# Four single PSUM banks in place of two double ones after the attention, in a one-core attention + RWKV-7 + FFN layer

## The chip, the cores and the metric

One core of one Trainium2 chip runs the whole layer as one program. The metric is the device time of that program in microseconds (us), the median of several runs. TensorE is called PE, VectorE DVE, ScalarE ACT, GpSimd POOL, and SP issues the DMAs.

## The reference

One layer over 16 meta tokens and 1024 inputs (1040 positions, width 1024), all in float32:

```python
def hybrid_mixer(hn, ...):
    q, k, v, f_logit, rw, gates = split(hn @ w_in)
    o_fox  = fox_attention(norm(q), norm(k), v, cumsum(log_sigmoid(f_logit)))   # 8 heads of 64
    y      = rwkv7_scan(r, decay, k, v, -kk, kk * a)                            # 8 heads of 64
    o_rwkv = (group_norm(y) + bonus) * g
    g_fox, g_rwkv = split(sigmoid(gates + g_b))
    return (g_fox * (o_fox @ w_bf) + g_rwkv * (o_rwkv @ w_br)) @ w_o

def conv_ffn(hn, w_up, w_conv, w_down):           # D_FF = 2816, conv of width 3 along time
    gate, val = split(causal_conv(hn @ w_up))
    return (silu(gate) * val) @ w_down

h = h + hybrid_mixer(rms_norm(h), ...);  h = h + conv_ffn(rms_norm(h), ...)
```

## The kernel before

**Data.** Activations lie transposed, 128 features on the partitions and time along the free axis, 1026 columns in three pieces (`CW`) of 342. To keep float32 accuracy each product is three matmuls of a rounded form (`mm3`, lines 212 to 220): high weight times high data, high weight times low data, low weight times high data. A product with 1024 inputs is 24 matmuls into one PSUM bank, called a group here; with 512 inputs 12. `wload` (line 194) fetches a weight tile `wf` of 256 KB, ACT rounds it to `wh` (line 205), POOL subtracts to get `wl` (line 206).

**Stages.** Stage 0 makes the projections. Then three streams are merged (`stage12`): `att` (attention, queries in blocks, whose scores need 1024 columns in one piece), `rec` (preparation, then the scan: 17 chunks of 64 steps, `rw_chain`) and `gat` (the gate projections, in three pieces for each of 16 weight tiles, written to DRAM as `sg`). A chunk is a chain on small tiles: eight products from the state `zb` (line 522), copy `pt` (ACT, 524), eight products (533), copies `uv` (ACT 534 and DVE 535), eight products (540), the next state (DVE, 543); sixteen products give the output (548, 550), which goes to DRAM as `y_d` (copy `yt`, 552). Each chunk loads the next one's tensors (`rw_load`): w, am and bkt of 256 KB and six of 64 KB, 1,152 KB. Gate products fill PE between the links. After the scan the third piece's group norm (`group_norm`, four times: a product with `bo64` at line 872, a square on ACT, a second product at line 877, and a chain to `orw`) and the load of the attention's result (`fox_load`, `ofx`) run beside stage 3, which makes `merged`. Stage 4 multiplies by `w_o`, adds the input and takes the norm: a sum over partitions (line 623), fourteen small DVE steps, a broadcast by PE into `st` (line 638), and per 128 features a scaled `x` (DVE, 1033), its rounding (ACT, 1035) and its rest (DVE or POOL, 1036). It does so for pieces 0 and 1, then for piece 2. Stage 5 makes for each of 22 tiles three column pieces of `ug` and `uv` (`conv`: a group, then ACT 1075 and DVE 1076 and 1077, all three reading the bank; then ACT 1088, DVE 1090, ACT 1092, POOL 1093) and, in between, the down products `dn` (512 columns).

**PSUM.** There are 8 banks of 512 float32 columns. The pool `S.pp` holds the tags S and M, each of two banks (1024 columns), and t, o, A and B of one. `banks(S, mm="S S M M t")` names the places that a kind of use takes in turn; `psum` (line 238) hands out the next. Two equal names in a row are the two halves of one tile, which is taken once for both:

```python
    if n and slots[n - 1] == t:
        return S.half[tag][:, 512:1024]
    S.half[tag] = slot(S, t, tag)
    return S.half[tag][:, 0:512]
```

So before, the gates run on S S M M, stage 3 on S S M M t o A, stages 4 and 5 on S S M M t; `gn` has t and o, `ch` A and B, `st` and `dn` o, A and B. Attention needs S and M whole.

**Order.** A scheduler orders each engine's instructions by a simulated timeline, with the order of the program as priority; it may move a group, or part of one, ahead of another where it thinks that the first would wait. A change of places thus changes the order as well.

Of the kernel before, what the change touches and what calls it, by code (L numbers as in the profile page):

```python
# [7 lines left out]
F32 = mybir.dt.float32  # L8
# [6 lines left out]
PSUM = bass.MemoryType.PSUM  # L15
DRAM = bass.MemoryType.DRAM

P = 128
# [208 lines left out]
def banks(S, **use):  # L227

    S.psb.update({k: v.split() for k, v in use.items()})
    S.psn.update({k: 0 for k in use})  # L230


def slot(S, tag, name):
    w = 1024 if tag in "SM" else 512
    return S.pp.tile([P, w], F32, name=name, tag=tag, bufs=1)


def psum(S, tag):

    slots = S.psb[tag]  # L240
    n = S.psn[tag] % len(slots)
    S.psn[tag] += 1
    t = slots[n]
# [4 lines that stand above are left out]
# [642 lines left out]
def stage12(S):  # L890

    nc, tc = S.nc, S.tc
    banks(S, mm="S S M M", st="t o", pr="A B", t="t", o="o")
    p1_cm = tc.tile_pool(name="p1", bufs=1, side="right")
    p1 = p1_cm.__enter__()
    S.smask = p1.tile([P, 384], BF16, name="smask")
    nc.gpsimd.memset(S.smask[:], 1.0)
    nc.gpsimd.memset(S.smask[:].rearrange("p (c t) -> p c t", t=64)[:, :, 0:1], 0.0)
    stage0(S)
    banks(S, mm="S M")  # L900
    S.op = S.rp = None
    S.scanned = False
    S.ev = 0

    def att():
        with tc.tile_pool(name="a", bufs=1) as ap:
            forget(S, ap)
            yield 12
            S.q2 = [[ap.tile([66, 348], F32R, name=f"q2{i}{e}") for e in range(2)] for i in range(3)]
            for i in range(3):  # L910
                for e in range(2):
                    nc.gpsimd.memset(S.q2[i][e][64:66, :].bitcast(F32), 1.0)
            for p in range(NP_):
                yield from attention(S, ap, p)
        S.op_cm = tc.tile_pool(name="op", bufs=1)
        S.op = S.op_cm.__enter__()
        S.orw = [[S.op.tile([P, LT], F32R, name="orw", bufs=8) for _ in range(2)] for _ in range(4)]
        banks(S, gate="S S M M", gn="t o", ch="A B", sv="A B")

    def rec():  # L920
        yield from prep(S, p1)
        p1_cm.__exit__(None, None, None)
        with tc.tile_pool(name="r", bufs=1, side="right") as rp:
            S.rp = rp
            banks(S, sv="A", ch="A", gate="B")
            if S.op is not None:
                banks(S, gate="S S M M", ch="A B", sv="A B")
            two = lambda nm: [[rp.tile([P, 4, 64], F32, name=f"{nm}{i}{e}") for e in range(2)] for i in range(2)]

            S.zb, S.arb = two("zb"), two("arb")  # L930
            for e in range(2):
                nc.gpsimd.memset(S.zb[0][e][64 * e:64 * e + 64], 0.0)
                for i in range(2):
                    nc.gpsimd.memset(S.arb[i][e][64 - 64 * e:128 - 64 * e], 0.0)
            S.at = {}
            yield from solve(S, 0)
            nxt = iter(())
            for c in range(NCH):
                if c % 6 == 0:
                    yield from nxt  # L940
                    nxt = solve(S, c // 6 + 1) if c < 12 else iter(())
                for t in rw_chain(S, c):
                    yield t
                    for _ in range(2):
                        next(nxt, None)
                if c in (5, 10):
                    while S.op is None:
                        yield 1.0
                    yield from group_norm(S, (5, 10).index(c))

        S.of_cm = tc.tile_pool(name="of", bufs=1, side="right")
        S.ofp = S.of_cm.__enter__()
        S.scanned = True
        yield from merge_streams([(0.0, 1.0, group_norm(S, 2)), (0.0, 1.0, fox_load(S))])

    def gat():
        while S.rp is None:
            yield 1.0
        yield from gates(S, range(13))

        while not S.scanned:
            yield 1.0
        yield from gates(S, range(13, 16))

    for _ in merge_streams([(0.0, 1.0, att()), (0.0, 1.2, rec()), (0.0, 1.0, gat())]):
        pass
# [17 lines left out]
def stage3(S):  # L984

    nc, tc = S.nc, S.tc
    banks(S, mm="S S M M t o A")
    op = S.ofp
    T = lambda name, bufs=1: op.tile([P, 342], F32, name=name, tag=name, bufs=bufs)
    S.mg = []  # L990
    sgs = {}

    def branch(m, br):
        wb = wload(S, S.A["w_br"][8 * br + m], 4)
        if len(S.mg) <= m and (m, 1 - br, 0) in sgs:
            S.mg.append([S.xp.tile([P, LT], F32R, name=nm, tag="x") for nm in ("mh", "ml")])
        for c, (t0, t1) in enumerate(CW):
            o = slice(t0 - T0, t1 - T0)
            ot = (S.ofox, S.orw)[br]
            sg = sgs[m, br, c] = T("sg", 12)  # L1000
            nc.sync.dma_start(out=sg[:], in_=S.sg_d[8 * br + m, :, o])
            nc.scalar.activation(out=sg[:], in_=sg[:], func=AF.Tanh, scale=0.5)  # L1002
            ps = psum(S, "mm")
            mm3(S, ps[:, :342], wb, [(ot[k][0][:, o], ot[k][1][:, o]) for k in range(4)])
            nc.vector.scalar_tensor_tensor(out=sg[:], in0=sg[:], scalar=1.0, in1=ps[:, :342],
                                           op0=ALU.add, op1=ALU.mult)
            mf = sgs.get((m, 1 - br, c))
            if mf is not None:
                h, l = S.mg[m]
                nc.vector.tensor_tensor(out=mf[:], in0=mf[:], in1=sg[:], op=ALU.add)  # L1010
                nc.scalar.activation(out=h[:, o], in_=mf[:], func=AF.Copy, scale=0.5)
                nc.vector.scalar_tensor_tensor(out=l[:, o], in0=mf[:], scalar=0.5, in1=h[:, o], op0=ALU.mult, op1=ALU.subtract)


    for m, br in [(0, 0), (1, 0), (0, 1), (1, 1)] + [(m, br) for m in range(2, KD) for br in range(2)]:
        branch(m, br)
    S.of_cm.__exit__(None, None, None)
    S.op_cm.__exit__(None, None, None)


def stage4(S):

    nc, tc = S.nc, S.tc
    banks(S, mm="S S M M t", st="o A B")
    S.h2 = [S.mp.tile([P, LT], F32, name="h2", tag="h", bufs=8) for _ in range(KD)]
    S.x2 = [[S.mp.tile([P, LT], F32R, name="x2", tag="x2", bufs=16) for _ in range(2)] for _ in range(KD)]
    with tc.tile_pool(name="p4", bufs=1) as p4:
# [10 lines left out]
        for cs in ((0, 1), (2,)):  # L1038
            acc = {}
            for m in range(KD):  # L1040
                w = wload(S, S.A["w_out"][m], KD)
# [14 lines left out]
            for c in cs:  # L1056
                st = psum(S, "st")
# [4 lines left out]
def stage5(S):  # L1062

    nc, tc = S.nc, S.tc
    banks(S, mm="S S M M t", dn="o A B")
    with tc.tile_pool(name="p5", bufs=1) as p5:

        def conv(w, mt, a, z, name):
# [52 lines left out]
def build(tc, A, outs):  # L1121
    S = K()
    S.nc = nc = tc.nc
    S.tc, S.A = tc, A
    with ExitStack() as ctx:
        cp = ctx.enter_context(tc.tile_pool(name="cst", bufs=1))
        dp = ctx.enter_context(tc.tile_pool(name="dram", bufs=1, space=DRAM))
        S.wp = ctx.enter_context(tc.tile_pool(name="w", bufs=1))
        S.xp = ctx.enter_context(tc.tile_pool(name="x", bufs=16))
        S.cp = cp  # L1130
        S.ar_d = dp.tile([NCH, P, 4, 64], F32, name="ar_d")
        S.w1_d = dp.tile([NCH, P, 8, 64], F32, name="w1_d")
        S.am_d = dp.tile([NCH, P, 8, 64], F32, name="am_d")
        S.a_d = dp.tile([3, NCH, 8, 32, 32], F32, name="a_d")
        S.x_d = dp.tile([2, NCH, 8, 32, 32], F32, name="x_d")
        S.bkt_d = dp.tile([NCH, P, 512], F32, name="bkt_d")
        S.v_d = dp.tile([LP, 512], F32, name="v_d")
        S.g_d = dp.tile([4, P, L], F32, name="g_d")
        S.bon_d = dp.tile([4, P, L], F32, name="bon_d")
        S.sw_d = dp.tile([4, P, L], F32, name="sw_d")  # L1140
        S.tha_d = dp.tile([4, P, L], F32, name="tha_d")
        S.y_d = dp.tile([4, P, L], F32, name="y_d")
        S.sg_d = dp.tile([16, P, LT], F32, name="sg_d")
        S.f_d = dp.tile([8, 2, L], F32, name="f_d")
        S.of_d = dp.tile([4, P, L], F32, name="of_d")
        S.outT = outs
        S.psb, S.psn, S.half = {}, {}, {}
        S.pp = ctx.enter_context(tc.tile_pool(name="ps", bufs=1, space=PSUM))
        stage12(S)
        stage3(S)  # L1150
        S.mp = ctx.enter_context(tc.tile_pool(name="mf", bufs=1))
        stage4(S)
        stage5(S)
# [81 lines left out]
```

## Time and profile before

| | |
|---|---|
| median of 3 runs | 1974.12 us (1974.03 to 1975.23) |
| the profiled execution: time, span | 1975.84 us, 1974.1 us |
| PE busy | 1851.5 us, 94% of the span |
| DVE, ACT, POOL busy | 884.0, 729.7, 604.6 us |
| mean granted PE clock | 0.968 |
| stage 0 and attention, about | 0 to 690 us |
| scan with gates, about | 690 to 965 us |
| end of the scan to stage 3 | 965 to 1025 us |
| stage 3 / stage 4 / stage 5, about | 1025, 1150, 1208 to 1974 us |

PE is busy nearly throughout, so what counts is the time in which PE stands still or runs at its lower clock. In a row of the timeline the bracket gives how long the engine was idle before the instruction and what ended that. Matmuls overlap: their starts, not their durations, say how fast they follow one another.

### The profile page before, as it was taken

How to read it: one execution, taken by the hardware profiler on the slowest of the kernel's cores; microseconds unless marked ns; L12 is line 12 of the kernel's file. 1: busy time of each engine (PE TensorE's matmuls, PEld its weight loads, DVE VectorE, ACT ScalarE, POOL GpSimd, SP SyncE). 2: the span in 40 equal slices, each digit the busy share in tenths (PEclk: the TensorE clock that was granted, in tenths of full speed). 3: DMA queues.
4: the chain of work that ended last, by engine and by line, in shares of the span. 5: the costliest groups of instructions: out<-in, count | busy, mean ns of one | idle time of the engine just before them, and what ended most of it. 6: DMA issues, size and time to landing. Idle time of an engine off the chain costs nothing.

```text
span 1974.1 us, 33238 instructions
## 1 busy us (share of the span) xinstructions
PE 1851.5 (94%) x12876; PEld 1660.5 (84%) x12876; DVE 884.0 (45%) x1804; ACT 729.7 (37%) x1608; POOL 604.6 (31%) x651
## 2 busy tenths in 40 slices
PE   6899998999998999999789998999999999999999
PEld 5588788788786788888679988898988989989997
DVE  6125636636727686333155465332332332433333
ACT  5335535436535432334454334331331322322221
POOL 5134124124225212233222343332332332322322
PEclk9899998999998999999989998999999999999999
DMA  5221331323412537666535331111111111111113
GB/s 186 85 70 44 84 93 47 80 74 85 102 50 68 136 87 193 162 187 178 162 97 150 110 125 60 39 50 47 43 48 38 44 56 41 54 48 38 49 44 106
DMA packets 197574, 170.82 MB, mean 87 GB/s; under 512 B 93768, under 2 KB 155768, under 8 KB 197416
## 3 DMA queue, kind: packets, MB, share of 16 engines
q1 hardware_dynamic: 197160, 168.62, 30.1%
q8 instruction: 102, 1.67, 0.4%
q14 instruction: 56, 0.46, 0.1%
q0 software_dynamic: 256, 0.07, 0.0%
HBM read 122.57 MB, written 46.06 MB: 85 GB/s over the span
## 4 chain that ended last, share of the span: by engine, by line
PE 44%; DVE 3%; ACT 2%; DMA 1%; issue 1%; POOL 0%; SPq 0%; POOLq 0%; ACTq 0%; DVEq 0%
PE mm L218 11%; PE mm L219 11%; PE mm L220 10%; PE dn L218 4%; PE dn L220 4%; PE dn L219 4%; DMA sg<-sg_d 0%; DVE uv L1076 0%; DMA y<-of_d 0%; POOL wl L206 0%; DVE ug L1076 0%; ACT L652 0%; DVE ry L633 0%; DVE x L1033 0%; ACT L1002 0%
## 5 line engine op out<-in xcount | busy, mean ns | idle before, releaser
L206 POOL TENSOR_TENSOR wl<-wf,wh 128x512 fp32r<-128x512 f32 (+1 forms) x268 | 347.0, 1298 | 592.6 <-ACT wh L205 583.7
L218 PE MATMUL mm<-x,wh 128*128 128x344 f32 (+1 forms) x1056 | 339.7, 323 | 12.7 <-DVE uv L1077 8.3
L219 PE MATMUL mm<-x,wh 128*128 128x344 f32 (+1 forms) x1056 | 340.4, 323 | 0.6 <-DVE x L1036 0.5
L220 PE MATMUL mm<-x,wl 128*128 128x344 f32 (+1 forms) x1056 | 335.9, 322 | 1.6 <-POOL wl L206 1.6
L205 ACT CAST wh<-wf 128x512 fp32r<-128x512 f32 (+1 forms) x268 | 163.7, 612 | 380.6 <-PE dn L219 168.6
L218 PEld LDWEIGHTS mm<-x,wh 128*128 128x128 f32 x1056 | 200.9, 190 | 16.9 <-issue 12.5
L219 PEld LDWEIGHTS mm<-x,wh 128*128 128x128 f32 x1056 | 200.9, 190 | 2.0 <-DVE x L1036 1.2
L220 PEld LDWEIGHTS mm<-x,wl 128*128 128x128 f32 x1056 | 200.2, 190 | 2.5 <-POOL wl L206 2.4
L1104 DVE TENSOR_TENSOR h<-h,dn 128x512 f32<-128x512 f32 x96 | 65.9, 688 | 168.9 <-PE dn L220 168.8
L218 PE MATMUL dn<-gh,wh 128*128 128x512 f32 x352 | 138.5, 394 | 0.1
L219 PE MATMUL dn<-gl,wh 128*128 128x512 f32 x352 | 138.5, 394 | 0.0
L220 PE MATMUL dn<-gh,wl 128*128 128x512 f32 x352 | 138.3, 394 | 0.0
L1093 POOL TENSOR_TENSOR gl<-ug,gh 128x342 fp32r<-128x342 f32 (+1 forms) x66 | 57.8, 877 | 254.5 <-ACT gh L1092 244.8
L218 PE MATMUL gate<-xh,wh 128*128 128x342 f32 x384 | 128.3, 337 | 2.9 <-ACT sg L855 2.2
L219 PE MATMUL gate<-xl,wh 128*128 128x342 f32 x384 | 125.8, 328 | 0.0
L220 PE MATMUL gate<-xh,wl 128*128 128x342 f32 x384 | 124.2, 326 | 0.0
L1076 DVE SCALAR_TENSOR_TENSOR ug<-mm,par,ug 128x342 f32<-128x342 f32 (+1 forms) x66 | 37.7, 572 | 186.3 <-ACT ug L1075 186.3
L218 PE MATMUL mm<-xh,wh 128*128 128x348 f32 (+5 forms) x336 | 117.1, 349 | 4.0 <-ACT xh L156 1.9
L219 PE MATMUL mm<-xl,wh 128*128 128x348 f32 (+5 forms) x336 | 114.4, 340 | 3.3 <-POOL xl L158 3.1
L220 PE MATMUL mm<-xh,wl 128*128 128x348 f32 (+5 forms) x336 | 112.8, 336 | 0.0
L1076 DVE SCALAR_TENSOR_TENSOR uv<-mm,par,uv 128x342 f32<-128x342 f32 (+1 forms) x66 | 37.5, 573 | 139.7 <-ACT uv L1075 139.4
L218 PE MATMUL pr<-xh,wh 128*128 128x386 f32 (+1 forms) x288 | 96.2, 334 | 1.4 <-ACT bt L468 1.4
(306 smaller groups left out, 4031.5 us busy)
## 6 DMA issues: line engine op xcount, KB each, us to landing
wf<-in_w_up_dram SPq DMA_DIRECT2D x88, 256.0 KB, 2.7
sg_d<-sg SPq DMA_DIRECT2D x48, 171.0 KB, 4.1
sg<-sg_d SPq DMA_DIRECT2D x48, 171.0 KB, 2.6
wf<-in_w_gate_dram SPq DMA_DIRECT2D x32, 256.0 KB, 3.8
wf<-in_w_out_dram SPq DMA_DIRECT2D x32, 256.0 KB, 2.8
wf<-in_w_down_dram SPq DMA_DIRECT2D x32, 256.0 KB, 2.7
wf<-in_w_rw_dram SPq DMA_DIRECT2D x28, 256.0 KB, 2.8
wf<-in_w_qkv_dram SPq DMA_DIRECT2D x24, 256.0 KB, 2.8
```

The lines of the kernel that those rows point to most:

```text
L205: nc.scalar.copy(out=wh[:, :n], in_=wf[:, :n])
L206: nc.gpsimd.tensor_tensor(out=wl[:, :n], in0=wf[:, :n], in1=wh[:, :n], op=ALU.subtract)
L218: nc.tensor.matmul(ps, lhsT=wh, rhs=xh, start=first and k == 0, stop=False)
L219: nc.tensor.matmul(ps, lhsT=wh, rhs=xl, start=False, stop=False)
L220: nc.tensor.matmul(ps, lhsT=wl, rhs=xh, start=False, stop=last and k == n - 1)
L1076: nc.vector.scalar_tensor_tensor(out=t[:, :n], in0=ps[:, 1:1 + n], scalar=cw(1), in1=t[:, :n], op0=ALU.mult, op1=ALU.add)
L1093: nc.gpsimd.tensor_tensor(out=gl[:, s], in0=g[:, :n], in1=gh[:, s], op=ALU.subtract)
L1104: nc.vector.tensor_tensor(out=hs, in0=hs, in1=ps[:], op=ALU.add)
```

## The change

S and M leave the pool `S.pp` for a pool of their own, `ps1`, which is closed when the attention stream ends. A pool `ps2` is opened in its stead, with four tags 0, 1, 2, 3 of 512 columns. From there on every use that had S S M M has 0 1 2 3: gates, stage 3 (0 1 2 3 t o A), stages 4 and 5 (0 1 2 3 t). No instruction of the kernel's work is added or removed. Lines of the changed file lie one to five further down.

```diff
 def slot(S, tag, name):
     w = 1024 if tag in "SM" else 512
-    return S.pp.tile([P, w], F32, name=name, tag=tag, bufs=1)
+    pool = S.pp if tag in "toAB" else S.pq
+    return pool.tile([P, w], F32, name=name, tag=tag, bufs=1)
...
+    pq_cm = tc.tile_pool(name="ps1", bufs=1, space=PSUM)
+    S.pq = pq_cm.__enter__()
...
             for p in range(NP_):
                 yield from attention(S, ap, p)
+        pq_cm.__exit__(None, None, None)
+        S.pq = S.ctx.enter_context(tc.tile_pool(name="ps2", bufs=1, space=PSUM))
...
-        banks(S, gate="S S M M", gn="t o", ch="A B", sv="A B")
+        banks(S, gate="0 1 2 3", gn="t o", ch="A B", sv="A B")
...
-                banks(S, gate="S S M M", ch="A B", sv="A B")
+                banks(S, gate="0 1 2 3", ch="A B", sv="A B")
...
-    banks(S, mm="S S M M t o A")
+    banks(S, mm="0 1 2 3 t o A")
...
-    banks(S, mm="S S M M t", st="o A B")
+    banks(S, mm="0 1 2 3 t", st="o A B")
...
-    banks(S, mm="S S M M t", dn="o A B")
+    banks(S, mm="0 1 2 3 t", dn="o A B")
```

What it does to the order shows in three places. The first is stage 5, ACT, the middle of a typical tile (mm_13983 and so on are PSUM tiles; two names after one tile, as ug_14069 and uv_14038 from mm_14013, are its two halves). Before:

```order
L1075 ACTIVATE uv_14038<-mm_14013,par_133 128x340
L1092 CAST gh_13981<-ug_14008 128x340
L1075 ACTIVATE uv_14099<-mm_14074,par_133 128x342
L1075 ACTIVATE ug_14069<-mm_14013,par_133 128x342
L205 CAST wh_14169<-wf_14167 128x512
L1088 ACTIVATE ug_14069<-ug_14069 128x342
```

and in the changed kernel:

```order
L1080 ACTIVATE ug_14068<-mm_14043,par_136 128x340
L1093 ACTIVATE ug_14068<-ug_14068 128x340
L1080 ACTIVATE uv_14098<-mm_14073,par_136 128x340
L1097 CAST gh_14041<-ug_14068 128x340
L1080 ACTIVATE ug_14130<-mm_14105,par_136 128x342
L1093 ACTIVATE ug_14130<-ug_14130 128x342
L1080 ACTIVATE uv_14160<-mm_14135,par_136 128x342
```

Before, the uv of the second column piece (uv_14099) is read out ahead of its ug (ug_14069), which is the second half of mm_14013; now ug and uv come strictly by turns, each from a bank of its own, and on PE the groups stand whole, one after the other, to the end of the program.

The second place is PE at the last norm of stage 4, which stands among the first groups of stage 5 (mm_13206, mm_13267). Before:

```order
L219 MATMUL mm_13206<-x2_12018,wh_13127 128x344
L220 MATMUL mm_13206<-x2_12017,wl_13128 128x344
L623 MATMUL st_13059<-ones_137,acc_12759 114x1 x3
L218 MATMUL mm_13206<-x2_12019,wh_13127 128x344
L219 MATMUL mm_13206<-x2_12020,wh_13127 128x344
L220 MATMUL mm_13206<-x2_12019,wl_13128 128x344
L638 MATMUL st_13059<-ident_135,ry_13064 128x114 x3
```

Changed, around the second of the two products (line 639 there):

```order
L219 MATMUL mm_13257<-x2_12060,wh_13177 128x344
L220 MATMUL mm_13257<-x2_12059,wl_13178 128x344
L639 MATMUL st_13109<-ident_138,ry_13114 128x114 x3
L218 MATMUL mm_13287<-x2_12045,wh_13183 128x344
L219 MATMUL mm_13287<-x2_12046,wh_13183 128x344
```

Between the two products of the norm stood 3 matmuls, and now stand 41 (the last 17 of one group and the 24 of mm_13257).

The third place is ACT at the end of the scan (pt, uv0 and yt are links of the chain, sg is the read-out of a gate group). Before, chunks 15 and 16:

```order
L524 COPY pt_10319<-ch_10310 128x256
L205 CAST wh_11064<-wf_11062 128x512
L855 ACTIVATE sg_10908<-gate_10856,par_133 128x342
L855 ACTIVATE sg_10948<-gate_10923,par_133 128x342
L534 COPY uv0_10186<-ch_10351 64x256
L552 COPY yt_10390<-ch_10373 128x256
L205 CAST wh_11120<-wf_11118 128x512
L524 COPY pt_10402<-ch_10393 128x256
L855 ACTIVATE sg_10975<-gate_10923,par_133 128x342
L205 CAST wh_11187<-wf_11185 128x512
L855 ACTIVATE sg_11003<-gate_10978,par_133 128x342
L534 COPY uv0_10296<-ch_10433 64x256
```

and changed:

```order
L856 ACTIVATE sg_11029<-gate_11004,par_136 128x342
L553 COPY yt_10312<-ch_10295 128x256
L525 COPY pt_10338<-ch_10329 128x256
L535 COPY uv0_10205<-ch_10371 64x256
L553 COPY yt_10410<-ch_10393 128x256
L525 COPY pt_10422<-ch_10413 128x256
L535 COPY uv0_10315<-ch_10453 64x256
```

The last gate group is read out in chunk 14, and on PE no gate matmul stands between the links of chunks 15 and 16. In the chunks ahead of these, PE has up to 60 gate matmuls per chunk where it had about 48.

## Rows read from the trace of the kernel before

**Rows 1.** The page's busy times by engine, and the shares of the chain that ended last.

```profile
PE 1851.5 (94%) x12876; PEld 1660.5 (84%) x12876; DVE 884.0 (45%) x1804; ACT 729.7 (37%) x1608; POOL 604.6 (31%) x651
...
PE 44%; DVE 3%; ACT 2%; DMA 1%; issue 1%; POOL 0%; SPq 0%; POOLq 0%; ACTq 0%; DVEq 0%
```

**Rows 2.** Windows by stage: from:to, length, then busy us (and instructions) of PE, PE's weight loads, DVE, ACT, POOL, then granted PE clock, DMA share, GB/s.

```profile
0.00:690.00 690.00, 623.02 (x4324) 523.67 (x4324) 366.07 (x812) 321.82 (x792) 224.85 (x306) 0.94 0.32 86
690.00:965.00 275.00, 266.15 (x3076) 236.29 (x3076) 131.25 (x304) 90.74 (x205) 74.92 (x81) 0.99 0.59 160
965.00:1025.00 60.00, 39.60 (x218) 32.96 (x217) 26.86 (x56) 39.81 (x71) 11.28 (x12) 0.87 0.47 137
...
1150.00:1218.00 68.00, 58.33 (x340) 54.97 (x338) 49.50 (x108) 28.80 (x57) 32.88 (x27) 0.92 0.32 102
1218.00:1620.00 402.00, 390.85 (x2235) 368.25 (x2236) 131.11 (x229) 115.11 (x223) 120.67 (x107) 0.99 0.15 45
1620.00:1974.00 354.00, 349.48 (x1919) 320.83 (x1917) 118.12 (x196) 88.24 (x171) 100.06 (x90) 1.00 0.17 54
```

**Rows 3.** The waits of PE from 1240 to 1960 us (stage 5): what waited for what, us in total, times, longest.

```profile
PE mm L218 <- DVE uv L1077: 8.3, 6, 1.8
PE mm L220 <- POOL wl L206: 1.6, 2, 0.8
PE mm L218 <- DVE ug L1077: 1.4, 5, 0.5
```

**Rows 4.** The timeline at one of the longest of these waits: start, us, what, and the idle time before.

```profile
1270.48 1.02 ACT L1075 ACTIVATE uv<-mm,par 128x340 f32<-128x340 f32 x2 [2.87 <-PE mm L220]
...
1271.06 1.05 DVE L1076 SCALAR_TENSOR_TENSOR uv<-mm,par,uv 128x340 f32<-128x340 f32 x2 [3.97 <-ACT uv L1075]
1272.03 1.04 DVE L1077 SCALAR_TENSOR_TENSOR uv<-mm,par,uv 128x340 f32<-128x340 f32 x2
1272.74 0.40 PE L218 MATMUL mm<-x,wh 128*128 128x344 f32 x1 [1.82 <-DVE uv L1077]
```

**Rows 5.** The timeline from stage 4 into stage 5, the norm of the third piece and the first wait behind it.

```profile
1203.06 0.67 PE L623 MATMUL st<-ones,acc 128*114 128x1 f32 x6
...
1206.54 0.92 PE L638 MATMUL st<-ident,ry 114*128 114x114 f32 x6 [2.24 <-DVE ry L633]
1207.50 1.53 DVE L1033 SCALAR_TENSOR_TENSOR x<-h,par,st 128x342 f32<-128x342 f32 x3 [1.02 <-PE st L638]
...
1214.72 1.19 POOL L1036 TENSOR_TENSOR x<-x,x 128x342 fp32r<-128x342 f32 x1
```

**Rows 6.** PE's idle times in stage 4 and behind it, in the timeline.

```profile
1174.99 0.92 PE L638 MATMUL st<-ident,ry 114*128 114x114 f32 x6 [0.75 <-DVE ry L633]
...
1181.41 0.42 PE L218 MATMUL mm<-mh,wh 128*128 128x342 f32 x1 [2.19 <-ACT wh L205]
...
1182.95 0.42 PE L220 MATMUL mm<-mh,wl 128*128 128x342 f32 x1 [0.97 <-POOL wl L206]
...
1208.63 0.65 PE L218 MATMUL mm<-x,wh 128*128 128x344 f32 x1 [1.17 <-ACT x L1035]
...
1218.20 0.63 PE L218 MATMUL mm<-x,wh 128*128 128x342 f32 x1 [1.66 <-DVE ug L1077]
```

**Rows 7.** Windows around the stretches of a lower clock (columns as in rows 2).

```profile
1034.00:1184.00 150.00, 145.23 (x925) 143.76 (x924) 85.71 (x159) 58.24 (x118) 55.16 (x42) 1.00 0.42 127
1184.00:1191.00 7.00, 7.00 (x37) 6.81 (x36) 5.44 (x11) 4.32 (x9) 5.06 (x5) 0.76 0.44 138
...
1208.00:1225.00 17.00, 14.16 (x58) 12.96 (x59) 9.67 (x20) 8.49 (x16) 4.62 (x4) 0.71 0.10 31
...
1436.00:1443.00 7.00, 7.00 (x35) 7.00 (x36) 1.16 (x3) 1.66 (x4) 3.07 (x3) 0.76 0.08 27
```

**Rows 8.** Two matmuls of one group in a row at the lower clock, and two at full clock: start, us.

```profile
1436.56 0.49 PE L218 MATMUL mm<-x,wh 128*128 128x344 f32 x1
1436.85 0.49 PE L219 MATMUL mm<-x,wh 128*128 128x344 f32 x1
...
1443.30 0.32 PE L218 MATMUL mm<-x,wh 128*128 128x344 f32 x1
1443.46 0.32 PE L219 MATMUL mm<-x,wh 128*128 128x344 f32 x1
```

**Rows 9.** The links of a chunk near the scan's end, in the timeline.

```profile
954.19 0.68 PE L533 MATMUL ch<-pt,at 64*64 64x64 f32 x16
...
955.45 0.43 DVE L535 COPY uv<-ch 64x256 f32<-64x256 f32 x1 [6.01 <-ACT uv L534]
...
962.84 0.69 PE L522 MATMUL ch<-zb,w 128*64 128x64 f32 x16
963.63 0.37 ACT L524 COPY pt<-ch 128x256 f32<-128x256 f32 x1 [0.63 <-PE ch L522]
```

**Rows 10.** The third piece's norms on PE between the scan and stage 3, in the timeline.

```profile
999.16 1.13 PE L872 MATMUL gn<-y,bo 128*128 128x342 f32 x2 [4.38 <-DMA y<-y_d]
1005.15 0.74 PE L877 MATMUL gn<-sq,bo 128*128 128x342 f32 x2
1013.30 0.84 PE L872 MATMUL gn<-y,bo 128*128 128x342 f32 x2 [0.83 <-DMA y<-y_d]
...
1016.79 0.74 PE L877 MATMUL gn<-sq,bo 128*128 128x342 f32 x2
```

More of the change, by code (lines that the diff above doesn't have):

```diff
@@ L1125, in build @@
     with ExitStack() as ctx:
+        S.ctx = ctx
         cp = ctx.enter_context(tc.tile_pool(name="cst", bufs=1))
```

## The prediction

> **What bounds the kernel now.** Read first the busy times: PE works in 94% of the span, no other engine in half of it, and PE has 44% of the chain, DVE 3% [rows 1]. So the time is PE's work plus the places where PE stands still or runs at its lower clock, and a change that alters no instruction of the work can only move those. The windows by stage show where: the scan has 266.15 busy of 275 us, the stretch behind it 39.60 of 60, stage 4 with the way into stage 5 58.33 of 68, stage 5 some 11 idle in its first 400 us and 4.5 in the rest [rows 2]; not all of that is a wait, since some matmul records are missing, so the waits view is taken for sizes: in stage 5 PE waits 8.3 us in six waits for the last read-out of a uv, 1.4 in five for that of a ug, 1.6 in two for a low weight [rows 3]. The timeline shows what such a wait is: PE ends a group, ACT, DVE and DVE again read it (two pieces at a time, about 0.5 us each), and only then, 1.82 us late, PE goes on [rows 4]. The reader is to see that PE has work and a place in PSUM is missing: the next group is the other half of a tile whose first half is still being read. The places are told apart as whole tiles only.
>
> **The change part by part.** All sums are made against the profiled execution's own 1975.84 us.
>
> *The waits in stage 5.* With five places that come free one by one, the changed order runs groups whole and by turns. A group is 24 matmuls at 0.16 us from start to start [rows 8], 3.8 us. Its place is wanted again after four others, some 15 us later; its read-out is ACT and twice DVE, half a us each [rows 4], so it is over long before, even behind a tile's whole queue. The 8.3 + 1.4 + 1.6 [rows 3] go: **-11.3 us**. The two waits for a low weight may stay, as may a few short ones for DVE: bounds -11.3 and -8.
>
> *From stage 4 into stage 5.* Here PE waits 2.24 for the norm's small steps on DVE, 1.17 for the first rounded x and 1.66 for the read-out of a first half [rows 5, 6], 5.07 us. The norm's small steps last from the end of line 623's products to 1206.5, some 2.8 us [rows 5]; the order now puts 41 matmuls there, 41 x 0.16 = 6.4 us, which hides them. What is late next: eight x go through DVE from 1207.5, two DVE steps of 0.5 each, until about 1215 [rows 5], and DVE's queue now has all of them ahead of any read-out of stage 5. The next 24 matmuls, 3.8 us, don't need them; the group after them takes one x per 3 matmuls, 0.47 us, and DVE makes one in about 0.95, so PE ends about 1 us late, and the first bank waits about 0.5 for its read-out behind the x. 1.5 of the 5.07 come back: **-3.6**, bounds -5.1 and +1 (all of the x's 7.6 us less the 6.4 that cover them).
>
> *Stage 4's second pass.* 0.75 for a norm's small steps goes, since those products are further apart, too; 2.19 and 0.97 for a weight behind ACT's and POOL's work on x [rows 6] have nothing to do with PSUM places, but the order around them moves. I take half of them: **-2.3**, bounds -3.9 and +3.2, another such wait.
>
> *The lower clock.* In three stretches the granted clock falls, to means of 0.76, 0.71 and 0.76 [rows 7], between the levels 1.2 and 2.4 GHz; each follows waits (1181 to 1183, 1206 to 1208 with 1218, and 1426 to 1436), and within such a stretch matmuls start 0.29 us apart instead of 0.16 [rows 8]. At full clock the 35 matmuls of the last would take 35 x 0.157 = 5.5 of its 7 us: 1.5 lost. In the same way 37 give 1.2 in the first, and 58 give 14.16 - 9.1 = 5.0 in the middle one. The last stretch goes with its waits; of the others I take half, as much as I took of their waits: **-4.6**, bounds -7.7 and 0.
>
> By the Trainium skill's page "TensorE: Matmul & The Clock Gate", section "A second HAM failure mode: psum-queue depth-cycling", a kernel that cycles through the PSUM banks idles a little between groups often enough for the clock to swing. That would speak against the change; it is rival D.
>
> *Scan.* The work is the same, but gate groups now run out in chunk 14. What hides a chunk's links in the others is gate matmuls; with none, PE waits from the end of line 522's products (963.53) to the end of pt (964.00), 0.47 us, and from the end of line 533's (954.87) to the end of uv (955.88), 1.0 us [rows 9]; the third link lies under the chunk's own sixteen output products. That is 1.5 a chunk, 3.0 for two, less some 0.5 that PE waited there before: **+2.5**. The lower bound is +1.5. The upper: chunk 16's 1,152 KB at the 160 GB/s that the scan reaches [rows 2] take 7.2 us against some 4.6 of a chunk without gates; two chunks late by 2.6 make it +8. In the chunks ahead the gates only lie denser; what they hid stays hidden. With the gates their 256 KB weights and their writes of sg move ahead in SP's queue, beside the chunks' loads; DMA is 0.59 busy there [rows 2], so I take that at nothing, and at the upper bound if it is not.
>
> *From the scan to stage 3.* The third and fourth norms' products stand 74 and 12 rows further down PE's queue, counted from the first norm's. So the 4.38 wait for y [rows 10] is covered, -4.4. But the second product of the third norm, which came 6.0 us after its first (999.16 to 1005.15), now has 3 matmuls in between, half a us: +5.5; the fourth's came 3.5 after its first [rows 10] and has 13 (2.0): +1.5. In all **+2.6**, bounds -4.4 and +7.
>
> *The opening of the pool, and stages 0 to attention.* No order of PE changes up to about 725 us, and S and M are whole there as before: 0. At the swap the gates' first tiles wait for the last scores to be read, as before, when the same tags were handed on: 0.
>
> Sum: -11.3 - 3.6 - 2.3 - 4.6 + 2.5 + 2.6 = -16.7, 1959.1 for an execution like the profiled one. The median before is 1.7 below that one, so **1957.5 us**.
>
> **The rivals.**
>
> *B, stage 5 alone gains.* What stage 4 loses is put down to x and weights, which remain, and the scan's end costs 5: -11.3 - 1.5 + 5 + 2.6 = -5.2, 1969 us. For it: DVE is busy 49.5 of 68 us there [rows 2] and its queue is the same. Against it: the 1.66 and 2.24 are of the kinds that the new order covers.
>
> *C, slower.* The norms between the scan and stage 3 take the place of what is removed. Their third now begins 74 matmuls later, 74 x 0.157 = 11.6 us; if the fourth then again follows by the 14.1 us that lay between their first products (999.16 to 1013.30) [rows 10], with nothing ahead of it in PE's queue, 25.7 us are lost where 2.6 were counted: 1957.5 + 23.1 = 1981. It decides as soon as the y of the fourth norm is fetched only when the third is done. Against it: only 2 to 3 matmuls separate these products in the order, so the planner counts on y being there; two y buffers exist.
>
> *D, slower by the clock.* The banks in rotation make PE idle between groups, and the clock in stages 3 to 5 falls to the mean of the first 690 us, 0.94 [rows 2]: 940 us x (1/0.94 - 1) = 60, so 2017. Against it: stage 3 turns over six places already and is granted 1.00 from 1034 to 1184 [rows 7]. By that section of the page the clock would swing; this trace does not agree so far, in groups that take turns without a wait.
>
> *E, no difference.* B with the scan's end and the norms at their bounds, +8 and +7: -11.3 - 1.5 + 8 + 7 = +2.2, with 4 of stage 4's: 1972 to 1976. That the change does nothing is excluded: the order differs from the end of attention on.
>
> **How the numbers follow.** Forecast 0.68, B 0.18, C 0.06, D 0.02, E 0.06. A measurement of this kernel can tell about 0.2%, 4 us, from no change: 1970.2 to 1978.1 is "same". Faster holds the forecast, and most of B, whose spread reaches over the edge: 0.84. Same is E and the rest of B: 0.09. Slower: C and D less a little that falls short, 0.07. The range: the terms' lower bounds together give -30.9, 1943 us, but hardly all at once, so 1946. The upper end takes in B, 1970. So 1946 to 1970; the forecast's own is 1948 to 1965.
>
> **What would show it.** Stage 5's waits for line 1082 (formerly 1077) under 2 us in all, and no stretch of low clock; in the way into stage 5 a wait of 1 to 2 us for x; idle of 1 to 1.5 a chunk in the last two chunks; PE idle for `gn` with a releaser of ACT or DVE instead of the DMA. It is wrong if those waits in stage 5 stay, with the same releaser (then the place was not the reason), or if the stretch from the scan to stage 3, 60 us long, grows by over 10.

## The result, and the profile after

The changed kernel takes 1951.14 us (median of 4 runs, 1943.5 to 1953.36) against 1974.67 for the kernel before: the ratio is 0.987, 95% interval 0.985 to 0.990. The forecast was 1957.5, in a range of 1946 to 1970. A second measurement of the same kernel gave 1944.57 (1939.78 to 1945.88), ratio 0.984 (0.982 to 0.986).

PE's busy time is that of before (1851.5 us [rows 1]); what went is time beside it. The page after, the span and the busy times:

```profile
span 1951.6 us, 33237 instructions
...
PE 1851.2 (95%) x12876; PEld 1662.3 (85%) x12876; DVE 884.5 (45%) x1804; ACT 733.5 (38%) x1608; POOL 602.9 (31%) x651
```

The windows of the changed kernel, columns as in [rows 2]:

```profile
725.00:960.00 235.00, 228.41 (x2641) 204.65 (x2640) 105.29 (x233) 78.41 (x167) 67.67 (x74) 0.98 0.61 166
960.00:975.00 15.00, 10.38 (x208) 8.95 (x206) 2.97 (x7) 4.17 (x10) 3.74 (x4) 1.00 0.68 189
975.00:1030.00 55.00, 42.70 (x197) 34.89 (x193) 26.48 (x55) 37.19 (x66) 10.54 (x11) 0.81 0.46 134
1034.00:1184.00 150.00, 148.45 (x951) 147.89 (x951) 84.30 (x159) 58.01 (x118) 54.37 (x42) 1.00 0.42 128
1184.00:1206.00 22.00, 19.63 (x121) 18.29 (x120) 14.14 (x32) 6.95 (x15) 11.15 (x9) 1.00 0.34 106
1206.00:1218.00 12.00, 9.85 (x60) 8.77 (x58) 8.69 (x17) 6.06 (x14) 3.35 (x3) 0.98 0.06 22
1218.00:1225.00 7.00, 6.54 (x24) 6.58 (x25) 4.89 (x10) 4.64 (x9) 4.63 (x4) 0.54 0.12 37
1225.00:1948.00 723.00, 722.33 (x4082) 675.41 (x4080) 244.47 (x414) 202.61 (x384) 216.92 (x193) 1.00 0.17 51
```

The last row is the one to see: in 723 us of stage 5 PE is busy for 722.33 at full clock, where before some 11 us of waits [rows 3] and a low stretch [rows 7] stood. One such stretch is left, at the entry into stage 5 (0.54 from 1218 to 1225).

Where the time went, step by step, is read best by laying two traces against each other by PE's work: for a moment of the trace before, the sum of all columns of matmuls still to come is taken (0.158 us per 344 columns, at least 0.04 each), and the moment at which the other trace has as much left; the growth of the difference from one moment to the next is what a stretch gained or lost. This is the ledger in what follows. For the full change and the experiments below, in us (minus is a gain; the boundaries are moments of the trace before; e5 is the full change again). Two of the boundaries, 725 and 1206.5, lie where the order moved or in the middle of a wait, so that neighbouring rows share a gain; the section on the prediction sets them elsewhere.

| stretch | full | e5 | e8 | e9 | e1 | e2 | e6 | e7 | e3 | e4 |
|---|---|---|---|---|---|---|---|---|---|---|
| 0 to 690, order as before | +3.2 | -3.1 | +1.8 | -3.9 | -4.5 | +1.2 | -0.5 | +9.7 | +3.0 | -2.0 |
| to 725, end of attention | +3.4 | +3.3 | +3.3 | +2.8 | +0.6 | +0.2 | +0.6 | +0.2 | +4.9 | +0.5 |
| to 960, scan | -3.2 | -8.0 | -4.0 | -7.6 | +2.5 | -0.5 | +5.8 | +2.3 | -8.1 | +2.9 |
| to 975, scan's end | +2.2 | +0.3 | +1.0 | +1.6 | -0.1 | +0.1 | 0.0 | +2.4 | +1.0 | -0.4 |
| to 1030, to stage 3 | -4.1 | -4.4 | -5.4 | -3.6 | +0.3 | -3.0 | -2.7 | -4.6 | +0.5 | -1.1 |
| to 1150, stage 3 | -1.2 | -1.2 | -1.0 | -1.2 | -0.3 | -1.1 | -1.1 | -1.1 | -0.2 | -0.9 |
| to 1206.5, stage 4 | -4.0 | -4.0 | -4.5 | -4.9 | -0.4 | -4.9 | -4.0 | -4.0 | +0.6 | -2.2 |
| to 1230, into stage 5 | -2.7 | -2.7 | +3.6 | -8.7 | -4.1 | -5.1 | -3.6 | -3.6 | +0.1 | +3.7 |
| to 1969, stage 5 | -16.3 | -16.5 | -16.6 | -15.4 | -16.6 | -16.6 | -16.6 | -16.6 | +0.1 | -16.6 |

### The profile page after: what moved, and what is told of

It is laid out like the page before. It is cut to its first block, busy times and chain, and to the rows that moved or that the text cites. A ratio compares the mean times of both kernels' runs of the same rounds, so it can differ in the third digit from the quotient of the medians.

```text
span 1951.6 us, 33237 instructions
## 1 busy us (share of the span) xinstructions
PE 1851.2 (95%) x12876; PEld 1662.3 (85%) x12876; DVE 884.5 (45%) x1804; ACT 733.5 (38%) x1608; POOL 602.9 (31%) x651
## 4 chain that ended last, share of the span: by engine, by line
PE 57%; DVE 2%; DMA 2%; ACT 1%; SPq 1%; issue 0%; POOL 0%; ACTq 0%; DVEq 0%
PE mm L218 11%; PE mm L219 11%; PE mm L220 11%; PE dn L218 4%; PE dn L220 4%; PE dn L219 4%; PE gate L218 3%; PE gate L219 3%; PE gate L220 3%; DMA y<-y_d 1%; PE ch L541 1%; DVE x L1041 1%; PE ch L534 0%; PE ch L523 0%; PE ch L551 0%
```

## The experiments

**e1, e2, e3: the parts alone.** In e1 and e2 the double places are kept longer (the pool `ps1` is closed before stage 5, or before stage 3, instead of when attention ends); in e3 `ps2` is closed after the scan and the double places come back.

```diff
 e1:  gates "S S M M", stage 3 "S S M M t o A", stage 4 "S S M M t", stage 5 "0 1 2 3 t"
 e2:  gates "S S M M", stage 3 "0 1 2 3 t o A", stages 4 and 5 "0 1 2 3 t"
 e3:  gates "0 1 2 3", stage 3 "S S M M t o A", stages 4 and 5 "S S M M t"
```

> Only stage 5 has the four single banks; gates and stages 3 and 4 keep the double places. Theory (waits for a half-read tile): the ledger by work done gives 16 us to stage 5, 11.3 of waits, about 0.2 for each of 13 restarts, 1.5 of low clock; so 1974.7 - 16 = 1958 to 1959, no wait of PE for the read-outs of uv and ug there. Rival (the gain is spread over the order of the whole program): under 8 us, 1967 or more.

> Gates keep the double places, stages 3 to 5 have the single ones. Theory: stage 5 (16) and stage 4 with the way into 5 (7) gain, the scan's end gives back nothing: the last chunks keep their gate matmuls, and the waits at the scan's start and for the first two group norms are those of before. 1974.7 - 23 = 1952, within 4. Rival (the gates' single banks are worth as much as they cost in chunk 15 and 16 and more): slower than the full change by 5 or more, 1956 up.

> Only the gates have single banks, stages 3 to 5 the double ones again. Theory: +5 at the scan's end, +4 where the pools change, -8 at the scan's start and its norms, -4 behind the scan: 1970 to 1977, no difference that can be told. Rival (the gate banks cost): over 1978; rival (they gain): under 1968.

e1: 1958.0 us (ratio 0.992, 0.989 to 0.995), as the theory had it: stage 5 alone gains 16.6 from its second tile on and 4.1 at the entry. e2: 1946.1 us (0.986, 0.983 to 0.988), some 6 under what was expected, and not slower than the full change. e3: 1977.34 us (1.001, 0.9995 to 1.003), with +1.0 at the scan's end where +5 was expected: the gates' banks alone can't be told from no change, and stage 5 waits as before, to the tenth (waits of PE in e3's stage 5, what waited for what, us, times, longest; line 1083 is line 1077 of before):

```profile
PE mm L218 <- DVE uv L1083: 8.3, 6, 1.8
PE mm L220 <- POOL wl L206: 1.6, 2, 0.8
PE mm L218 <- DVE ug L1083: 1.4, 5, 0.5
```

The waits for a low weight, which have nothing to do with PSUM by name, belong to the same order: they are here, and gone wherever stage 5 has independent places.

**e4, e8: fewer places.** e4 is the kernel before with one line changed, e8 the full change with one.

```diff
 e4:
-    banks(S, mm="S S M M t", dn="o A B")
+    banks(S, mm="S M t", dn="o A B")
 e8:
-    banks(S, mm="0 1 2 3 t", dn="o A B")
+    banks(S, mm="0 1", dn="o A B")
```

> The kernel before with one line changed: stage 5 takes S, M and t by turns, each tile whole, with half of S and M unused: three places instead of five halves. Theory (a half that waits for its other half): with three independent places a group's place is wanted again 7.6 us after it is full and read out in under 3, so all the waits go, as with five: 1958 to 1960. Rival (the number of places counts): waits return every third group, 1974 or more.

> The full change with two places (0 1) instead of five in stage 5. Theory: from stage 5's second tile on a place is wanted again 3.8 us after its group ends and is read out in 1.7 when nothing is queued ahead, so the 16 us stay gained, all but a few; at the entry into stage 5, where DVE's queue has the eight x ahead of the first read-outs, PE waits 10 to 15. In all 8 to 18 slower than e5. Rival (a queue of PSUM places as deep as possible is what counts): waits at every group, 1985 or more.

e4: 1959.65 us (0.991, 0.989 to 0.994); e8: 1954.11 (0.989, 0.986 to 0.991), 9.5 above e5 on the same chip. From 1230 on both gain 16.6, with three places and with two, as much as with five. So it is not the number of places that stage 5 lacked: half of what S and M hold is thrown away in e4, and the waits are gone. They came from two groups sharing one tile.

The kernel before shows the same, wait by wait, when the rows of its trace are laid against the order of its program. Each of the eleven waits for a read-out [rows 3] stands at the first matmul into the first half of a tile, and it ends about 0.15 us after the last read-out of the second half of the tile that had the same two banks before. The bank of the first half itself had been read out 8.8 to 9.8 us earlier. At 1272.74 [rows 4] that is bank 6, read out by 1263.49, while the read-out of its neighbour ends at 1272.59. So a bank was free, and the tile that it is half of was not. The order of the groups changed together with the places in all these runs, so what the order alone did is not shown.

What fewer places cost is the entry alone, +3.7 and +3.6 where the full change has -2.7, by one wait of 10.0 us in each. ACT and PE in e4's timeline:

```profile
1216.27 0.54 ACT L1075 ACTIVATE ug<-mm,par 128x340 f32<-128x340 f32 x1 [1.02 <-POOL x L1036]
...
1218.52 0.63 PE L218 MATMUL mm<-x,wh 128*128 128x344 f32 x1 [10.04 <-DVE ug L1077]
```

ACT and DVE come to the first read-out only when the eight x of the last norm are done; until then PE can fill as many places as there are free ones.

**e5, e6: the full change and e2 again, on one chip.**

> The full change once more, beside e6 on the same chip, to have the two against each other and a second trace of the stretch up to 690 us, whose PE order is that of before. Theory: the 3.2 us that the full change lost there were the clock's play from run to run: they vanish or turn; the 3.4 at the change of pools, the 2 to 5 at the scan's end and the 16.3 of stage 5 from its second tile on stay, within 1 us each. Time 1947 to 1954.

> Double places for the gates, single banks from stage 3 on, once more beside the full change. Theory: 4 to 7 us faster than e5, since it has neither the lost microseconds where the pools change under the attention nor chunks without gate matmuls. Rival (chance): within 2 us of e5.

1944.57 and 1945.75 us (0.984, 0.982 to 0.986, and 0.986, 0.983 to 0.988): the rival has it, the gates' single banks neither cost nor gain what these runs could tell. The trace of e5 shows why the expected 4 to 7 didn't come: the 3.3 up to 725 is there, but the scan's end, expected at 2 to 5, shows 0.3, the scan gained 8.0, and e5 itself came out under its 1947 to 1954. In the traces with single banks for the gates (full, e3, e5, e8, e9) the scan's row is -3.2 to -8.1, in those in which the gates have the places of before (e1, e2, e4, e6) -0.5 to +5.8, and in e7 (two whole places for the gates) +2.3. Counted from 740 on instead of 725 it is -3.9 to -8.1 in the first five. I had put that at nothing; its cause stays open.

**e7: two whole places for the gates.** e2 with one line (twice) changed.

```diff
-        banks(S, gate="S S M M", gn="t o", ch="A B", sv="A B")
+        banks(S, gate="S M", gn="t o", ch="A B", sv="A B")
```

> As e6, but the gates take S and M by turns, each whole: two independent places and no change of pools before stage 3. The order is then, as in the full change, 22 gate matmuls per link, and chunk 16 and most of chunk 15 have none. Theory (independent places make the scheduler use up the gates early, however many there are): +2 to +5 at the scan's end against e6, nothing at 690 to 740. Rival (the change of pools is what costs): no difference from e6 at the scan's end.

1948.96 us (0.988, 0.985 to 0.990). The scan's end shows +2.4, and 690 to 725 shows +0.2: independent places make the gates run out early, and what is lost around 725 comes with the change of pools, not with independent places as such. The total is within the play of the others.

**e9: a sixth place.** After e4 and e8 only the entry into stage 5 wanted places.

```diff
-    banks(S, mm="0 1 2 3 t", dn="o A B")
+    banks(S, mm="0 1 2 3 t A", dn="o B")
```

> The full change with A as a sixth place for the groups of stage 5 and two places (o B) for the down products. Theory: only the entry into stage 5 still lacks a place (1.66 us, then a low stretch of 7 us, in the full change's trace); the sixth takes that wait and the low stretch with it: the ledger from 1206 to 1230 of before goes from -2.7 to between -5 and -8; from 1230 on nothing changes (-16.5), since there no wait is left, and two places are enough for the down products. So 2 to 5 us under the full change, 1941 to 1948. Rival (down products need three places): waits at them, 16 per pass, 1950 or more.

1941.29 us (median of 5, 1935.1 to 1950.98; ratio 0.985, 0.982 to 0.988), the lowest median of all, though its interval overlaps that of the full change: a gain over that is shown by the trace, not by the times. The entry's row is -8.7 where the full change has -2.7, and the low stretch at 1218 is gone (windows of e9):

```profile
1180.00:1225.00 45.00, 44.03 (x281) 43.25 (x280) 25.38 (x57) 20.22 (x41) 18.26 (x17) 1.00 0.15 47
1225.00:1900.00 675.00, 675.00 (x3839) 633.79 (x3839) 227.01 (x386) 193.22 (x367) 208.06 (x185) 1.00 0.16 48
```

About 1 us is given back near the end, where one down product waits for its place, 0.78 us at 1926.84 for line 1109.

## Why the prediction was right, step by step

**Stage 5: the mechanism held, the term was too small.** Forecast -11.3 and 1.5 for the low stretch, measured -16.3 to -16.6. Mis-sized was the price of a wait: the bracket's idle time was taken for all of it. The timeline of PE in the kernel before, around the wait of [rows 4]:

```profile
1270.60 0.32 PE L220 MATMUL mm<-x,wl 128*128 128x344 f32 x1
...
1272.97 0.32 PE L219 MATMUL mm<-x,wh 128*128 128x344 f32 x1
```

From 1270.60 to the start at 1272.74 [rows 4] there are 2.14 us where 0.16 is the rule [rows 8], a loss of 1.98 for an idle time of 1.82; and the next start follows after 0.23 instead of 0.16. A stop thus costs its idle time and about 0.24 more, since the matmul before it can no longer overlap with the next. For the 13 waits [rows 3] that is 3.1: 11.3 + 3.1 + 1.5 = 15.9 of 16.3 to 16.6; some 0.5 stays open. That the shared tile was the cause is shown by e3 (waits back), by e4 (waits gone without any new bank) and by the two halves at each wait, told above. One detail was the other way round: the group that waits in stage 5 is a first half, and what is still being read is the second half of the tile before it.

**Into stage 5.** Forecast -3.6, and 2.5 of the middle low stretch, -6.1 in all; measured -2.7 by the table. But 1206.5 lies at the end of the norm's wait of 2.24 [rows 5], which the forecast counts here and the table counts in stage 4. With the border ahead of that wait, at 1204 of before, the rows of stage 4 and of the entry are -1.5 and -5.2 in the full change, -2.5 and -7.5 in e2, -2.5 and -11.1 in e9, +2.0 and -6.5 in e1, +0.3 and +1.2 in e4. So the entry was over-rated by 0.9. The broadcast of the norm waits no longer, and the x are as late as reckoned; but the place is waited for by 1.66 us and not 0.5. The changed kernel:

```profile
1206.67 0.82 PE L639 MATMUL st<-ident,ry 114*128 114x114 f32 x6
...
1215.45 0.43 PE L219 MATMUL mm<-x,wh 128*128 128x344 f32 x1 [0.92 <-DVE x L1041]
1216.20 0.55 ACT L1080 ACTIVATE ug<-mm,par 128x340 f32<-128x340 f32 x1 [1.77 <-POOL x L1041]
...
1217.75 0.56 DVE L1082 SCALAR_TENSOR_TENSOR ug<-mm,par,ug 128x340 f32<-128x340 f32 x1
...
1218.45 0.63 PE L218 MATMUL mm<-x,wh 128*128 128x344 f32 x1 [1.66 <-DVE ug L1082]
```

ACT starts the first read-out at 1216.20, after all of the norm, though its group ended long before; DVE is through at 1218.3. What I had left out is that ACT's queue, not only DVE's, has the x ahead. Behind that stop the clock fell to 0.54 [the window 1218 to 1225 above], so that of the low stretch less came back than half. e9 shows both: with a sixth place the row is -8.7, 6.0 better, of which the 1.66, 0.24 for the restart, the 0.92 for x and the low stretch (24 matmuls, 3.8 us at full clock, in 6.54 busy: 2.7) make 5.5. The 2.7 may come without a sixth place: in e2 PE makes the same stop (1.65 us for the same read-out, at 1214), the granted clock stays at 1.00 from 1211 to 1225, and the row is -5.1.

**Stage 4.** Forecast -2.3 and 0.6 of clock, -2.9 in all; measured -1.5 with the border at 1204 (-4.0 by the table). It was over-rated by 1.4. The 2.19 for a weight [rows 6] is gone from the trace, and 0.37 of the norm's 0.75 is left, so that at 1185 of before the full change is 5.2 ahead. But new waits for weights follow, and at 1203 all but 1.2 of this is given back. PE's waits for a low weight in the whole changed kernel, all four between 1181 and 1197 (us, times, longest):

```profile
PE mm L220 <- POOL wl L206: 3.0, 4, 1.2
```

Of this kind there was one wait in stage 4 before, the 0.97 [rows 6]. e1 and e4, whose stage 4 has the old places, show no gain up to 1204 (+2.0 and +0.3).

**Scan's end.** Forecast +2.5, measured +2.2 and +0.3 in the two traces of the full change, +1.0 in e8 and e3, +1.6 in e9 and +2.4 in e7. The links stand bare as described, with one wait for a load of chunk 16 that I had kept for the upper bound:

```profile
966.13 0.68 PE L534 MATMUL ch<-pt,at 64*64 64x64 f32 x16 [0.82 <-ACT pt L525]
967.28 1.08 PE L541 MATMUL ch<-uv,bkt 128*64 128x64 f32 x15 [0.47 <-ACT uv L535]
971.04 0.68 PE L523 MATMUL ch<-zb,w 128*64 128x64 f32 x14 [1.24 <-DMA zb<-v_d]
972.23 0.68 PE L534 MATMUL ch<-pt,at 64*64 64x64 f32 x16 [0.52 <-ACT pt L525]
```

**From the scan to stage 3: the step that failed.** Forecast +2.6, measured -3.6 to -5.4. PE in the changed kernel:

```profile
980.63 0.84 PE L873 MATMUL gn<-y,bo 128*128 128x342 f32 x2 [1.06 <-DMA y<-y_d]
...
1009.09 0.74 PE L873 MATMUL gn<-y,bo 128*128 128x342 f32 x2
1012.45 0.42 PE L218 MATMUL mm<-orw,wh 128*128 128x342 f32 x1 [2.46 <-ACT orw L886]
1012.88 1.51 PE L878 MATMUL gn<-sq,bo 128*128 128x342 f32 x2
1015.78 1.48 PE L873 MATMUL gn<-y,bo 128*128 128x342 f32 x2 [0.82 <-DMA y<-y_d]
...
1026.03 0.60 PE L218 MATMUL mm<-orw,wh 128*128 128x342 f32 x2 [2.10 <-ACT orw L886]
```

The 4.38 for y [rows 10] is covered, as foreseen. But the 6.0 us between a norm's two products, which I took for the time that the second must wait, was a distance in PE's queue, filled with other work: now 3.8 us lie between them (1009.09 to 1012.88), of which 2.46 are idle and have another releaser, `orw`. So the loss is about 4.6 (2.46 + 2.10) beside what was gained, and I had not counted that the first norm's wait and that for `ofx` at 987 shrink, too: PE's waits for `ofx` in the changed kernel and in the one before (us, times, longest):

```profile
PE mm L218 <- ACT ofx L983: 2.5, 3, 1.4
```

```profile
PE mm L218 <- ACT ofx L978: 6.5, 1, 6.5
```

e3 (+0.5) against e2 and e6 (-3.0, -2.7) shows that it comes with stage 3's places, not with the gates'.

**What had no term.** The change of pools under the attention costs time, and I had it at 0. The table's border at 725 lies among gate groups that moved. From 722, up to which PE's order is that of before, to 740 the ledger gives +3.8 (full), +2.8 (e5), +4.0 (e8), +1.3 (e9) and +0.3 (e3), and 0.0 in the five traces without that change. Changed kernel, then before:

```profile
730.65 0.66 PE L218 MATMUL gate<-xh,wh 128*128 128x342 f32 x1 [1.82 <-ACT pb L786]
```

```profile
728.78 0.43 PE L218 MATMUL gate<-xh,wh 128*128 128x342 f32 x1 [0.60 <-ACT pb L785]
```

The first gate product waits 1.82 us for ACT's read-out of the last scores instead of 0.60 (0.86 in e3), and behind it three matmuls of a gate group take 0.85 us (731.67 to 732.52) where full clock gives 0.47. In e9, behind the same 1.82, the granted clock stays at 1.00 (723 to 731), and little more than the stop is lost. Before, sixteen gate matmuls (723.88 to 726.60) stood ahead of this wait, in the two banks of the attention tile that was free, while the last scores went to the other tile; in the changed kernel the first place of `ps2` lies in the banks of the last scores. Whether `ps2` needs both tiles read, or only its first place lay badly, no run tried. In e3 the scan's -8.1 outweighs what is lost up to 725 (+4.9) and at the scan's end (+1.0), but the -2.2 that is left does not show in its times, so that the gates' part comes out at nothing.

**The sum.** Forecast -16.7, measured -22.7 by the ledger. Stage 5 (with its low stretch) was under-rated by 3.5, the way to stage 3 by 6.7; stage 4 and the entry were over-rated by 1.4 and 0.9; without a term were the way to 725 with the change of pools (+3.4), the scan (-3.2), stage 3 (-1.2) and the first 690 us (+3.2), whose order no one touched. The largest term held in kind; that the sum came out so near is in part luck, by errors of both signs.

**The rivals.** D, the clock that falls with banks in rotation, is refuted here: 1.00 over 723 us with five places in turn, and in e4 over 715 with three. The Trainium skill's page "TensorE: Matmul & The Clock Gate" ("A second HAM failure mode: psum-queue depth-cycling") tells of a kernel in which PE idles a little between its groups and the clock swings. That case did not arise here: PE was busy for 722.33 of 723 us while its groups took turns. C did not come: the stretch behind the scan got shorter. B and E are out: stage 4 and the entry together gained 6.7, and the scan's end cost at most 2.4, not 5 or 8.

## What to carry to other kernels

Two accumulation groups that share one tile wait for each other's read-out; two small independent places do as well as five for a steady stream (e8), so look first at what is tracked as one, and only then at how many there are. The number counts where the read-out engines come late in a lump, as at the entry of a stage. Price a stop of PE by its start-to-start distance, not by the idle time in the bracket, and don't take a distance between two instructions in a queue for the time that the second has to wait. When two traces are compared stretch by stretch, set the borders where the order has not moved and no wait is cut in two.

## What the runs showed of the hardware

A stop of PE cost about 0.24 us more than its idle time, and one of 1.66 us was followed by 7 us at a mean granted clock of 0.54. Whether the clock falls behind such a stop differs from run to run: behind the 1.65 us of e2 at the same place it stayed at 1.00; behind the 1.82 us at the change of pools it was 0.60 in the full change (730 to 738) and 1.00 in e9 (723 to 731). The stretch up to 690 us, with one and the same order on PE, differed from run to run by -4.5 to +9.7 us. Its windows in e7 (the slowest there) and e9 show the granted clock at 0.92 and 0.94:

```profile
0.00:690.00 690.00, 627.54 (x4284) 524.61 (x4285) 359.39 (x789) 319.46 (x784) 220.01 (x304) 0.92 0.31 83
```

```profile
0.00:690.00 690.00, 623.75 (x4353) 523.27 (x4354) 371.30 (x823) 323.54 (x797) 222.48 (x306) 0.94 0.32 87
```

In e7's 690 us PE got through 4284 matmuls, in e9's 4353. With such play, differences of 5 us between two versions are seen in the ledger by stretches and not in the medians.
